# Low parts of 22 weight blocks of a two-layer hybrid trunk: formed by transfers that add into SBUF instead of subtractions on VectorE, with a new order of issue

## The chip, the cores and the metric

The kernel runs on one core of one Trainium2 chip. The metric is the device time of one execution in microseconds (us). Engines are named as in the profile: PE is TensorE's matmuls and PEld its weight loads, DVE is VectorE, ACT is ScalarE, POOL is GpSimd, SP is SyncE, which here only issues transfers. SBUF is the core's working memory, PSUM the eight banks in which PE accumulates, HBM the chip's main memory.

## The reference

Two layers over x of 1024 positions by 1024 channels, in float32. Shortened:

```python
for l in range(2):
    h = rmsnorm(x, attn_norm[l])
    proj = h @ w_in[l]            # one projection, columns split among four mixers
    (c_q, c_kv, k_r, g_b, g_c, u_conv, u_pool, q_sw, k_sw, v_sw) = split(proj)
    y_a = mla_attention(c_q, c_kv, k_r, ..., w_uq[l], w_ukv[l])   # 4 heads, causal, rotary
    y_b = short_gated_conv(g_b, g_c, u_conv, conv_w[l])           # width 3
    y_c = multiscale_pool(u_pool, pool_w[l], pool_scale[l])       # windows 2, 4, 8, 16
    y_d = swa_sink_attention(q_sw, k_sw, v_sw, sinks[l], slopes)  # window 128, ALiBi
    mixed = rmsnorm of each of the four, times mix_norm[l]
    x = x + mixed @ w_o[l]
    gate, up = split(rmsnorm(x, ffn_norm[l]) @ w_gate_up[l])
    x = x + (silu(gate) * up) @ w_down[l]
return rmsnorm(x, final_norm)
```

## The kernel before

**Three matmuls for one.** PE multiplies operands of the rounded format fp32r. To keep float32 accuracy every operand is held as two fp32r tiles, `hi` (the value rounded) and `lo` (the value minus `hi`), and `mm3` (L289) issues three matmuls for each product: hi·hi, hi·lo and lo·hi. For activations `split` makes the pair: `hi` by an ACT copy (L305), `lo` by a DVE subtraction (L306). L308 and L309 are the same with a gain multiplied in.

**Weights of the mixers.** `weights` (L220) loads one block of w_in (128x1024, 512 KB) or w_o (128x768, 384 KB) from HBM, forms `hi` with an ACT copy (L237) and `lo` with a DVE subtraction (L238). Small blocks (up to 256 columns) take a pool of their own. `expect_layer` lists the blocks of a layer in the order in which they will be needed, `ahead` fetches the next one and `take` hands it out. Each block's two tiles stand in a ring of two blocks. The weights of the feed-forward part (`w_gate_up`, `w_down`) go other ways: a factored scheme of sums and differences of blocks, whose sums are formed by POOL (L172) and DVE.

**Stages of one layer.** Input projection; the mixers (their scores in banks `ps_s`, their outputs in `ps_pv`, transposes in `ps_t`); `values` (from L1131 on), which computes MLA's v from its latent, copies it out of `ps_mm` as hi (ACT, L1155) and lo (DVE, L1156); output projection; feed-forward. Layer 0 takes the profile's stretch from 0 to about 1050 us with its mixers up to about 410, layer 1 from 1050 on with its mixers up to about 1410.

**The last stage.** At the very end of layer 1 the down projection's last unit accumulates four 128-row tiles, in two halves of 256 columns, in four banks (two `ps_t`, two `ps_mm`). `evac` (L1882) adds each finished half to x on DVE. The program writes the first half of all four and then the second half of all four.

**What sets the order.** The program's order is not the order of issue. At the end `order_engines` groups the instructions by PSUM bank and engine, gives each group a rank from the place in the program plus a number from the table `MOVES`, and fixes the order of every engine (SP's and POOL's transfer queues too) by that rank. Every engine then runs its list strictly in that order and waits at an instruction whose inputs are not ready.

**Buffers.** SBUF tiles named `u` are 47 places of 128x1024 that go round; the number behind a name in a listing (u7_131) is place and allocation. So a tile can also have to wait until the place's last reader is done.

Of the kernel before, what the change touches and what calls it, by code (L numbers as in the profile page):

```python
# [122 lines left out]
def trunk_kernel(ctx: ExitStack, tc: tile.TileContext, ins, out):  # L123
# [84 lines left out]

    def ring_next():

        if len(ring) == 2:
            ring_drop()
        ring.append((R.pair(), R.pair()))
        return ring[-1]
# [2 lines left out]
        for i in ring.popleft():  # L217
            R.free_pair(i)

    def weights(src, n, between=None):  # L220
        cuts = [slice(0, n // 2), slice(n // 2, n)] if between else [slice(0, n)]
        if n > 2 * P:
            s = F.pair()
            raw = F.ap2(s)
            if between:
                between()
            for c in cuts:
                sp.dma_start(raw[:, c], src[:, c])
            hi, lo = (R.ap2(i) for i in ring_next())
            F.free_pair(s)  # L230
        else:
            raw = wpool.tile([P, 2 * P], F32, name="vraw", tag="vraw")
            sp.dma_start(raw[:, :n], src)
            hi = wpool.tile([P, 2 * P], F32R, name="vhi", tag="vhi")
            lo = wpool.tile([P, 2 * P], F32R, name="vlo", tag="vlo")
# [23 lines left out]
    def expect_layer(l):  # L259
        for m in (2, 3, 0, 4, 5, 6, 1, 13, 14, 10, 11, 12, None, 7, 8, 9) if l == 0 else (14, 10, 11, 12, None, 7, 8, 9):  # L260
            if m is None:
                expect(rope_weights, l)
            else:
                begin = [first_loads] if (l, m) == (0, 2) else []
                expect(weights, ins["w_in"][l, m], 2 * HT, *begin)
        for d in range(NK):
            expect(weights, ins["w_o"][l, d], 6 * P)

    def ahead():
        if stream and not fetched:  # L270
            f, args = stream.popleft()
            fetched.append(f(*args))

    def take():
        ahead()
        return fetched.popleft()

    def pair_weights(src):
# [1859 lines left out]
def arrange(steps, rank=lambda v: v.rank):  # L2138
# [138 lines left out]
    return out  # L2277

MOVES = {
# [63 lines left out]
}  # L2343


# [161 lines left out]
```

## Time and profile before

| | |
|---|---|
| device time, median of 3 runs | 2034.13 us (2032.77 to 2035.87) |
| span of the profiled execution | 2031.1 us, first to last instruction |
| PE | 2014.0 us busy, 9378 matmuls |
| DVE | 1644.2 us busy |
| ACT | 1030.7 us busy |
| POOL | 210.7 us busy |
| transfers | 320.21 MB, mean 158 GB/s |
| granted TensorE clock | 0.998 |

The profiled execution is one of its own; its device time is not listed apart from its span, and the runs' median lies 3.0 us above that span. The profile's rows name engine, line, operation and tiles (out<-in) with buffer numbers left out. A row "PE ps_mm L294 <- DVE u L1156: 2.6, 2, 1.8" in the list of waits says that PE's matmuls of L294 into a bank ps_mm waited for the DVE instruction of L1156, 2.6 us in total, twice, 1.8 at the longest. Line numbers are those of the kernel before; in the changed kernel the same lines stand 16 further down (L294 is L310, L305 is L321, L1882 is L1898), except that L237 and L238 become L252 and L253.

### The profile page before, as it was taken

How to read it: one execution, taken by the hardware profiler on the slowest of the kernel's cores; microseconds unless marked ns; L12 is line 12 of the kernel's file. 1: busy time of each engine (PE TensorE's matmuls, PEld its weight loads, DVE VectorE, ACT ScalarE, POOL GpSimd, SP SyncE). 2: the span in 40 equal slices, each digit the busy share in tenths (PEclk: the TensorE clock that was granted, in tenths of full speed). 3: DMA queues.
4: the chain of work that ended last, by engine and by line, in shares of the span. 5: the costliest groups of instructions: out<-in, count | busy, mean ns of one | idle time of the engine just before them, and what ended most of it. 6: DMA issues, size and time to landing. Idle time of an engine off the chain costs nothing.

```text
span 2031.1 us, 26457 instructions
## 1 busy us (share of the span) xinstructions
PE 2014.0 (99%) x9378; PEld 1669.4 (82%) x9378; DVE 1644.2 (81%) x2793; ACT 1030.7 (51%) x1803; POOL 210.7 (10%) x212
## 2 busy tenths in 40 slices
PE   9999999999999999999999999999999999999998
PEld 7887888878888888888888878888888888888887
DVE  7889989998888888655778999899977777886555
ACT  7447656763333335443545676667333233355342
POOL 0000000013212213000000000000322222220000
PEclk9999999999999999999999999999999999999999
DMA  5100223346666667875455112231644454497652
GB/s 185 55 27 34 75 87 111 126 141 228 211 217 228 217 232 256 304 241 174 148 176 167 39 41 99 89 127 58 218 161 145 159 182 147 157 325 261 198 175 88
DMA packets 163781, 320.21 MB, mean 158 GB/s; under 512 B 13248, under 2 KB 85056, under 8 KB 163648
## 3 DMA queue, kind: packets, MB, share of 16 engines
q1 hardware_dynamic: 163648, 318.51, 45.6%
q8 instruction: 74, 1.21, 0.2%
q14 instruction: 59, 0.48, 0.1%
HBM read 220.41 MB, written 98.04 MB: 157 GB/s over the span
## 4 chain that ended last, share of the span: by engine, by line
PE 93%; DVE 3%; ACT 2%; DMA 1%; issue 1%; SPq 0%; DVEq 0%; ACTq 0%
PE ps_mm L294 37%; PE ps_s L294 28%; PE ps_t L294 11%; PE ps_pv L294 8%; PE ps_pv L1289 2%; PE ps_t L1277 2%; PE ps_s L1223 1%; PE ps_s L1224 1%; PE ps_s L1225 1%; PE ps_pv L814 1%; PE ps_s L753 1%; PE ps_mm L1109 1%; PE ps_t L802 1%; DVE u L346 1%; DVE u L306 1%
## 5 line engine op out<-in xcount | busy, mean ns | idle before, releaser
L294 PE MATMUL ps_mm<-u,u 128*128 128x512 f32 (+1 forms) x3402 | 856.6, 388 | 2.3 <-ACT u L237 1.3
L294 PEld LDWEIGHTS ps_mm<-u,u 128*128 128x128 f32 x3402 | 621.7, 188 | 126.8 <-issue 3.1
L294 PE MATMUL ps_s<-u,u 128*128 128x512 f32 x2628 | 651.2, 389 | 0.0
L294 PEld LDWEIGHTS ps_s<-u,u 128*128 128x128 f32 x2628 | 492.6, 188 | 104.2 <-DVE te L1796 0.8
L305 ACT CAST u<-u 128x1024 fp32r<-128x1024 f32 (+2 forms) x400 | 344.3, 883 | 412.1 <-PE ps_s L294 82.1
L306 DVE TENSOR_TENSOR u<-u,u 128x1024 fp32r<-128x1024 f32 (+2 forms) x400 | 412.7, 1049 | 165.2 <-ACT u L305 127.3
L172 POOL TENSOR_TENSOR u<-u 128x256 f32<-128x256 f32 x176 | 204.3, 1162 | 743.0 <-DMA u<-in_w_dn 239.2
L294 PE MATMUL ps_t<-u,u 128*128 128x512 f32 (+1 forms) x1142 | 275.1, 378 | 1.2 <-ACT u L305 0.8
L294 PEld LDWEIGHTS ps_t<-u,u 128*128 128x128 f32 x1142 | 205.5, 188 | 42.1 <-DVE u L306 1.3
L294 PE MATMUL ps_pv<-u,u 128*128 128x512 f32 x696 | 172.9, 389 | 0.0
L294 PEld LDWEIGHTS ps_pv<-u,u 128*128 128x128 f32 x696 | 130.5, 188 | 27.5 <-ACT tn L458 0.3
L1604 ACT ACTIVATE tp<-tp 128x512 f32<-128x512 f32 x84 | 53.3, 634 | 117.1 <-DVE tp L372 116.8
L1286 POOL MEMSET u<- 128x128 f32 x32 | 6.2, 220 | 858.8 <-DVE te L372 623.7
L305 ACT CAST u<-ps_t 128x512 fp32r<-128x512 f32 (+4 forms) x136 | 64.9, 507 | 58.7 <-PE ps_t L1277 34.1
L306 DVE TENSOR_TENSOR u<-ps_t,u 128x512 fp32r<-128x512 f32 (+4 forms) x136 | 77.0, 584 | 13.6 <-ACT u L305 12.7
L308 ACT ACTIVATE u<-u,par 128x512 fp32r<-128x512 f32 x100 | 70.0, 719 | 34.0 <-DVE u L372 10.9
L309 DVE SCALAR_TENSOR_TENSOR u<-u,par,u 128x512 fp32r<-128x512 f32 x100 | 73.1, 752 | 4.5 <-ACT u L308 4.4
L1605 DVE TENSOR_TENSOR tp<-tp,u 128x512 f32<-128x512 f32 x84 | 62.6, 745 | 13.2 <-ACT tp L1604 12.7
L340 ACT ACTIVATE tn<-u 128x512 f32<-128x512 f32 (+1 forms) x92 | 53.3, 594 | 39.0 <-DVE u L1882 30.2
L458 ACT COPY tn<-ps_s 128x512 f32<-128x512 f32 x66 | 38.4, 582 | 62.8 <-PE ps_s L294 62.5
L372 DVE TENSOR_TENSOR tp<-tp,u 128x512 f32<-128x512 f32 x80 | 60.9, 761 | 1.1
L1289 PE MATMUL ps_pv<-u,u 128*128 128x512 f32 (+2 forms) x184 | 54.4, 358 | 0.0
(220 smaller groups left out, 2171.9 us busy)
## 6 DMA issues: line engine op xcount, KB each, us to landing
u<-in_w_gu SPq DMA_DIRECT2D x88, 512.0 KB, 3.6
ad<-u SPq DMA_DIRECT2D x154, 256.0 KB, 2.8
u<-ad SPq DMA_DIRECT2D x70, 512.0 KB, 4.9
u<-in_w_dn SPq DMA_DIRECT2D x68, 512.0 KB, 4.9
qd<-u SPq DMA_DIRECT2D x44, 512.0 KB, 3.0
u<-qd SPq DMA_DIRECT2D x32, 512.0 KB, 4.9
u<-in_w_in SPq DMA_DIRECT2D x29, 512.0 KB, 3.5
u<-ws SPq DMA_DIRECT2D x28, 512.0 KB, 3.5
```

Of the source, the lines that this page charges most:

```text
L172: pool.tensor_tensor(out=o, in0=o, in1=u, op=ALU.add)
L294: pe.matmul(o, w, r, start=start and k == 0 and i == 0, stop=stop and k == n - 1 and i == 2, skip_group_check=again,)
L305: act.copy(hi, f)
L306: dve.tensor_tensor(out=lo, in0=f, in1=rd(hi), op=ALU.subtract)
L308: act.activation(hi, f, AF.Copy, scale=gain)
L309: dve.scalar_tensor_tensor(out=lo, in0=f, scalar=gain, in1=rd(hi), op0=ALU.mult, op1=ALU.subtract)
L340: act.activation(q, f, AF.Square)
L372: dve.tensor_tensor(out=o, in0=a, in1=b, op=ALU.mult)
L1277: pe.transpose(p[:, b * P : (b + 1) * P], pr[b][j // 4][:, (j % 4) * P : (j % 4 + 1) * P], ident,)
L1289: pe.matmul(py[:, c0:], v_of(j, h), R.ap(s)[:, c0:], start=j == 0 and n == 0, stop=j == nj - 1 and n == 1,)
L1604: last_silu = act.activation(g, g, AF.Silu)
L1605: dve.tensor_tensor(out=g, in0=g, in1=r, op=ALU.mult)
```

## The change

For 22 of the blocks that `weights` makes, `lo_left` takes the place of copy and subtraction. ACT copies the loaded block to `hi`, as before. Then ACT writes minus `hi` over the loaded block (`raw`). POOL's queue issues a transfer that reads the block from HBM again and adds it into `raw`, which then holds the value minus `hi`. SP's queue issues a transfer from `raw` to the tile `lo`. The waits between these four steps are by semaphores; the instruction that waits is POOL's issue (on ACT), SP's issue (on the adding transfer) and PE's matmul (on the copying transfer). The 22 blocks are eight of w_in of layer 0, two of w_in of layer 1, and of w_o the blocks d = 2 to 7 of both layers. The ring now holds one block more than those fetched and not handed out, and `ahead` may fetch two when more than seven places are free.

```diff
     def ring_next():
-        if len(ring) == 2:
+        while len(ring) > len(fetched) + 1:
             ring_drop()
...
+    def lo_left(src, raw, hi, lo, n):
+        act.copy(hi[:, :n], raw[:, :n])
+        act.activation(raw[:, :n], rd(hi[:, :n]), AF.Copy, scale=-1.0)
+        pool.dma_start(raw[:, :n], src, accum_op=ALU.add)
+        sp.dma_start(rd(lo[:, :n]), raw[:, :n])
+
-    def weights(src, n, between=None):
+    def weights(src, n, between=None, on_chip=False):
         cuts = [slice(0, n // 2), slice(n // 2, n)] if between else [slice(0, n)]
+        if n > 2 * P and not on_chip:
+            s = F.pair()
+            raw = F.ap2(s)
+            sp.dma_start(raw[:, :n], src)
+            hi, lo = (R.ap2(i) for i in ring_next())
+            F.free_pair(s)
+            lo_left(src, raw, hi, lo, n)
+            return hi, lo
...
-                expect(weights, ins["w_in"][l, m], 2 * HT, *begin)
+                expect(weights, ins["w_in"][l, m], 2 * HT, begin, m not in (0, 4, 5, 6, 1, 13, 14, 10))
         for d in range(NK):
-            expect(weights, ins["w_o"][l, d], 6 * P)
+            expect(weights, ins["w_o"][l, d], 6 * P, None, d < 2)
 
     def ahead():
-        if stream and not fetched:
+        while stream and (not fetched or len(fetched) < 2 and len(slots.places) > 7):
             f, args = stream.popleft()
             fetched.append(f(*args))
 
     def take():
-        ahead()
+        if not fetched:
+            ahead()
         return fetched.popleft()
...
 MOVES = {
-    3: -1110, 4: -1104, 5: -984, 7: -776, 8: -1105, 14: -914, 15: -964, 16: -307, 18: -279, 20:
+    0: -809, 1: -2, 2: 234, 3: -1340, 4: -1290, 5: -1134, 6: 506, 7: 34, 8: -1130, 9: -443, 10: 398,
```

The table `MOVES` is new from end to end, with several times as many entries. What it moves is seen in the orders of issue. In the rows below stand the line, the operation, the tile written <- the tiles read, the shape, and how many alike follow one another.

Place B, the start of layer 1, block m = 14 of w_in. ACT before; u32_10018 is the loaded block, u16_10020 its hi:

```order
L458 COPY tn_9858<-ps_mm_9843 128x512
L308 ACTIVATE u31_9993<-u14_9757,par_75 128x512
L830 COPY tn_9838<-ps_pv_9786 64x256
L305 CAST u11_9897<-ps_t_9892 128x512
L237 CAST u16_10020<-u32_10018 128x1024
L776 ACTIVATE tp_9940,sm2_9937<-ps_s_9931,sm2_9936 128x256 x2
```

ACT now, with u15_10046 the loaded block and u23_10048 its hi:

```order
L846 COPY tn_9866<-ps_pv_9814 64x256
L222 CAST u23_10048<-u15_10046 128x1024
L474 COPY tn_9886<-ps_mm_9871 128x512
L223 ACTIVATE u15_10046<-u23_10048 128x1024
L846 COPY tn_9866<-ps_pv_9814 64x256
```

The negation stands behind a copy out of the bank ps_mm, and SP's copy of the low part, u14_10049, among loads:

```order
L1060 DMA u13_9785<-in_rope_k 128x512
L232 DMA u7_10054<-in_w_in 128x1024
L995 DMA u13_9785<-xs_85 128x512
L225 DMA u14_10049<-u15_10046 128x1024
L243 DMA u43_10062<-in_w_in 128x1024
L995 DMA u13_9785<-xs_85 128x512
L225 DMA u36_10057<-u7_10054 128x1024
```

On PE the low part of that block, u11_10021 before, is first read here:

```order
L294 MATMUL ps_mm_9725<-u22_9174,u37_9856 128x512 x3
L294 MATMUL ps_mm_10030<-u4_8420,u16_10020 128x512 x2
L294 MATMUL ps_mm_10030<-u4_8420,u11_10021 128x512
L294 MATMUL ps_mm_10030<-u28_8660,u16_10020 128x512 x2
L294 MATMUL ps_mm_10030<-u28_8660,u11_10021 128x512
```

and now here, behind six matmuls of the sliding-window scores and two of another block with the high part:

```order
L310 MATMUL ps_mm_10068<-u12_8448,u23_10048 128x512 x2
L769 MATMUL ps_s_10145<-u46_10005,u37_9396 128x128
L769 MATMUL ps_s_10145<-u26_10006,u37_9396 128x128
L769 MATMUL ps_s_10299<-u46_10005,u37_9396 128x256
L769 MATMUL ps_s_10299<-u26_10006,u37_9396 128x256
L769 MATMUL ps_s_10173<-u46_10005,u37_9396 128x256
L769 MATMUL ps_s_10173<-u26_10006,u37_9396 128x256
L310 MATMUL ps_mm_10093<-u42_10021,u23_10048 128x512 x2
L310 MATMUL ps_mm_10068<-u12_8448,u14_10049 128x512
```

The matmuls with the high part and the first one with the low part, neighbours before, are now eight matmuls apart.

Place A, the output projection of layer 1, ACT now (before, one L237 stood there alone); u4_11638 is the loaded block, u34_11640 its hi:

```order
L321 CAST u15_11607<-ps_t_11605 128x128
L222 CAST u34_11640<-u4_11638 128x768
L1320 COPY tn_11614<-ps_pv_11537 64x512
L321 CAST u30_11778<-ps_t_11773 128x512
L223 ACTIVATE u4_11638<-u34_11640 128x768
```

Copy and negation are two steps apart, and the negation is what POOL's transfer waits for. The last matmul into ps_pv_11537 is the one that the COPY of L1320 waits for; PE's first use of the low part u7_11641 comes 55 matmuls behind it.

The last stage, PE before, where the first half of the bank ps_t_16744 ends:

```order
L294 MATMUL ps_t_16744<-u37_17571,u32_17588 128x256 x3
L358 MATMUL ps_pv_17697<-u1_16955,ones_77 128x512
L294 MATMUL ps_t_16802<-u43_17436,u39_17640 128x256
L294 MATMUL ps_t_16802<-u12_17437,u39_17640 128x256
L294 MATMUL ps_t_16802<-u43_17436,u13_17642 128x256
```

and now, where the same bank is called ps_t_16788 (a half's sum begins with u21_17480 and ends with u6_17615):

```order
L310 MATMUL ps_t_16788<-u6_17615,u13_17632 128x256 x2
L374 MATMUL ps_pv_17741<-u35_16999,ones_77 128x512
L310 MATMUL ps_t_16788<-u6_17615,u13_17632 128x256
L310 MATMUL ps_t_16788<-u21_17480,u45_17631 128x256
L310 MATMUL ps_t_16788<-u44_17481,u45_17631 128x256
```

Before, the next 99 matmuls went to the other three banks before this bank's second half began; now the second half begins at once. The bank ps_t_16846 (ps_t_16802 before) has the same. The two banks ps_mm keep three other halves between theirs.

More of the change, by code (lines that the diff above doesn't have):

```diff
@@ L263, in expect_layer @@
             else:
-                begin = [first_loads] if (l, m) == (0, 2) else []
-                expect(weights, ins["w_in"][l, m], 2 * HT, *begin)
+                begin = first_loads if (l, m) == (0, 2) else None
+                expect(weights, ins["w_in"][l, m], 2 * HT, begin, m not in (0, 4, 5, 6, 1, 13, 14, 10))
         for d in range(NK):
-            expect(weights, ins["w_o"][l, d], 6 * P)
+            expect(weights, ins["w_o"][l, d], 6 * P, None, d < 2)
     def ahead():
-        if stream and not fetched:
+        while stream and (not fetched or len(fetched) < 2 and len(slots.places) > 7):
             f, args = stream.popleft()
```

444 rows, old and new, of the table MOVES are left out of this document.

## The prediction

> **What bounds the kernel now.** The page's first part was read first, then the list of waits of TensorE, then the table by stage, and last the single lines and transfers that the change touches. The columns of the first part are busy time, share of the span and instructions.
>
> ```profile
> span 2031.1 us, 26457 instructions
> PE 2014.0 (99%) x9378; PEld 1669.4 (82%) x9378; DVE 1644.2 (81%) x2793; ACT 1030.7 (51%) x1803; POOL 210.7 (10%) x212
> ```
>
> TensorE (PE) is busy for 2014.0 of 2031.1 us and the number of its matmuls does not change. Time can only be won where PE waits, or lost where it is made to wait anew. The list of its waits (total, times, longest) is short:
>
> ```profile
> PE ps_mm L294 <- DVE u L1156: 2.6, 2, 1.8
> PE ps_mm L294 <- ACT u L237: 1.3, 1, 1.3
> PE ps_pv L198 <- DVE ones L145: 1.1, 1, 1.1
> PE ps_mm L294 <- ACT u L305: 1.0, 1, 1.0
> PE ps_t L294 <- ACT u L305: 0.8, 1, 0.8
> PE ps_s L360 <- ACT tn L1961: 0.5, 1, 0.5
> PE ps_t L294 <- DVE u L306: 0.3, 1, 0.3
> PE ps_s L1223 <- ACT u L305: 0.3, 1, 0.3
> ```
>
> They sum to 7.9 us. L198 and L237 (2.4 us) are the start, before the first data is there, and L1961 (0.5) is the very end; the change touches none of these three. So 5.0 us (2.6 + 1.0 + 0.8 + 0.3 + 0.3) is the most that a relieved VectorE (DVE) or ScalarE (ACT) can give back. The table by stage (first the stretch, then its length and the busy time of PE, PEld, DVE, ACT, POOL) shows where DVE is tight: in the mixers, which is where the 22 blocks are.
>
> ```profile
> 150.00:230.00 80.00, 78.21 (x365) 62.65 (x364) 76.35 (x147) 60.70 (x120) 0.35 (x2) 1.00 0.12 42
> 230.00:410.00 180.00, 180.00 (x897) 149.89 (x896) 165.28 (x360) 121.82 (x259) 2.69 (x14) 1.00 0.30 104
> 1050.00:1200.00 150.00, 149.97 (x740) 123.35 (x739) 132.90 (x321) 94.15 (x214) 0.00 (x0) 1.00 0.30 95
> 1200.00:1230.00 30.00, 28.88 (x139) 23.38 (x138) 29.88 (x62) 20.81 (x46) 0.35 (x2) 1.00 0.17 57
> ```
>
> DVE is 92 to 99% busy there, and yet PE loses almost nothing: 0.00 of 180 us, 0.03 of 150. The granted clock is 1.00, so nothing is to be won there.
>
> **Removed and added, engine by engine.** Ten of the blocks are 128x1024, twelve 128x768.
>
> ```profile
> L237 ACT CAST u<-u x39: 607/1037/1058, 6.2 to 1327.5; 128x1024 fp32r<-128x1024 f32 x21, 128x768 fp32r<-128x768 f32 x16, 128x512 fp32r<-128x512 f32 x2
> L238 DVE TENSOR_TENSOR u<-u,u x39: 685/1215/1228, 7.3 to 1328.4; 128x1024 fp32r<-128x1024 f32 x21, 128x768 fp32r<-128x768 f32 x16, 128x512 fp32r<-128x512 f32 x2
> L308 ACT ACTIVATE u<-u,par 128x512 fp32r<-128x512 f32 x100 | 70.0, 719 | 34.0 <-DVE u L372 10.9
> ```
>
> The durations are ns, shortest, median and longest. DVE loses 10 subtractions of 1.22 us and 12 of about 0.95 (between the 0.685 of 512 columns and the 1.215 of 1024): 23.6 us. ACT gains 22 negations. A 512-wide ACTIVATE takes 0.719 against 0.607 for the CAST of that width, so 0.11 more than a CAST: 10 x 1.15 + 12 x 0.93 = 22.7 us. Neither enters the sum as such. What covers them is PE's own work, 180.00 of 180 us in the second row of the table; ACT has 58 us to spare there. If DVE had been what PE waits for, the 23.6 us would show, but only 5.0 us of waits exist. The 5.0 us are at places (L1156, the split of v, for the most part) whose order, matmul then copy then subtraction then matmul, is the same after the change; I take the gain there as 0, with 5.0 as its bound. The new order might also let a wait of this kind in elsewhere; the largest that exists, 1.8 us, is my bound on that side.
>
> **The new path of a low part.** Before it was load, copy on ACT, subtraction on DVE (1.2 us), use. Now it is load, copy, negation on ACT, a second transfer of the block from HBM that adds into the negated copy (POOL's queue), a third transfer from SBUF to SBUF (SP's queue), use. The prices of the nearest transfers (size, median us from issue to landing):
>
> ```profile
> u<-in_w_in SPq DMA_DIRECT2D x29, 512.0 KB, 3.5
> u<-in_w_o SPq DMA_DIRECT2D x16, 384.0 KB, 3.1
> u<-in_w_kr SPq DMA_DIRECT2D x2, 256.0 KB, 2.6
> u<-in_xT SPq DMA_DIRECT2D x16, 256.0 KB, 5.4
> u<-in_w_in SPq DMA_DIRECT2D x2, 256.0 KB, 6.2
> L172 POOL TENSOR_TENSOR u<-u x176: 729/1072/2930, 432.7 to 1811.7; 128x256 f32<-128x256 f32 x176
> ```
>
> The third transfer is taken at the price of a load, 3.5 us (512 KB) or 3.1 (384 KB). The accumulating one has no row in this trace. From below it is bounded by the same plain loads, 3.1 and 3.5; from above by the dearest loads of a loaded queue, 6.2 at half the size, and I let the range run to 7. It has to read a second stream, the negated copy. From 256 to 512 KB a load grows by 0.9 us (2.6 to 3.5), so 512 KB more cost 1.8 and 384 KB more 1.35: 5.3 and 4.45. POOL, which issues it, has its instructions lengthened by 0.34 us in the median next to a busy DVE (1.072 against the shortest, 0.729); with that I take 5.7 and 4.8, near the middle of the bounds.
>
> The Trainium skill speaks against this change more strongly. Its page "SBUF — State Buffer" (the warning on the "DVE blocks DMA" trap in the section on the doors) says that descriptors of a transfer issued from GpSimd's queue are made by that engine's cores and cannot be written while a DVE operation holds the port pair that the two share. That POOL's additions stretch to 2.9 us agrees in kind, but no run here has such a transfer. By that rule the result is the second rival below.
>
> **Where the price meets PE.** What matters is the lead: the PE work between the end of a negation and the first matmul that uses the low part. Four rows price that work: the first two columns are start and duration.
>
> ```profile
> 1979.82 7.64 PE L294 MATMUL ps_pv<-u,u 128*128 128x512 f32 x33
> 1987.30 4.12 PE L294 MATMUL ps_t<-u,u 128*128 128x256 f32 x33
> 1991.25 1.02 PE L358 MATMUL ps_pv<-u,ones 128*128 128x512 f32 x2
> 1991.45 0.42 DVE L1882 TENSOR_TENSOR u<-u,ps_t 128x256 f32<-128x256 f32 x1 [1.20 <-PE ps_t L294]
> ```
>
> 33 matmuls of 512 columns start 7.48 us apart from the next group, 0.227 each; 33 of 256 take 3.95 to the next start, 0.120 each. With these I counted the lead of all 22 blocks along the new order. Eleven have more than 12 us and drop out, since 5.7 + 3.5 = 9.2 is under it. The short ones:
> - Place B, start of layer 1 (u15_10046, 512 KB). The negation follows a COPY of ps_mm for which PE waits at its next matmul on that bank. From there to the first use of u14_10049 PE has 12 matmuls of 512 (2.72 us) and 38 mixed ones (6.05), 8.8 in all; minus 1.1 for the negation 7.7; minus 3.5 for the third transfer, 4.2 are left for the accumulation. At 5.7 PE waits 1.5 us.
> - Place C, the very first such block (u7_131). ACT's cast of u34_334 comes right behind its negation, and from the matmul that reads u34_334 to the use of u9_134 PE has 38 matmuls of 0.227, 8.6 us; with the cast (0.6) and the signal 9.4; minus 3.5, 5.9 are left. Transfers at the start are slower: 256 KB of x take 5.4 us against 2.6 for as much later. Half of that 2.8 on top of 5.7 makes 7.1: PE waits 1.2 us.
> - Place A and its like, output projection (u4_11638, 384 KB): 55 matmuls, 11.0 us, from the last ps_pv matmul before it; minus 2.2 for the COPY, a cast and the negation on ACT, 8.8; minus 3.1, 5.7 are left against a price of 4.8. No wait. The tightest of these blocks (u39_2461) has 8.2 − 3.1 = 5.1; the others 5.5 to 7.1.
>
> All other transfers are hidden by such leads; their added traffic, 22 x about 1 MB in some 700 us of mixers, meets queues that are 0.12 to 0.30 busy in the table above.
>
> **The tail.** This term needs no new price. In the last stage the order before runs both banks' first column halves before any second half. The new order puts the second half (256 columns) of a ps_t bank directly behind its first half, twice. The second half's first matmul must wait until DVE has evacuated the first. By the rows above: the next matmul starts 1991.25 today; the evacuation ends at 1991.45 + 0.42 = 1991.87. The way from DVE's end to PE's start is read here:
>
> ```profile
> 223.13 0.42 DVE L1156 TENSOR_TENSOR u<-ps_mm,u 128x256 fp32r<-128x256 f32 x1
> 223.69 0.36 PE L294 MATMUL ps_mm<-vhi,u 128*128 128x256 f32 x1 [1.79 <-DVE u L1156]
> ```
>
> 223.69 − 223.55 = 0.14, so PE would start at 1992.01 and loses 0.76 us; twice 1.5 us. (In the first of the two the matmul of L374 stands one matmul ahead of the end of the first half, so it fills nothing.)
>
> **The sum.** 0 for the relieved engines, 1.5 (B) + 1.2 (C) + 0 (A) + 1.5 (tail) = +4.2 us. The profiled execution has a span of 2031.1, which becomes 2035.3; the median of the runs, 2034.13, lies 3.0 above that span for what is around it, so the time is 2038.4. About 0.2% (4.1 us: 2030.1 to 2038.2) is what a measurement of this kernel can tell from no change, and the forecast stands just outside.
>
> **Rivals.**
> - The accumulation is cheap, 4.2 us or less at either size. Then B and C are hidden and only the tail is left: 2035.6, no measurable change. For it: loads of this size take 3.1 to 3.5. Against it: the second stream. Chance 0.24.
> - The accumulation is dear, 7 us at either size, as where POOL is held up by DVE by more than the median. Then B costs 2.8, C 2.5, u39_2461 1.9, and the eight other short leads 0.2 to 1.5 each, 7 together: 14.2 + 1.5 tail = 15.7, 2049.8. For it: DVE 92 to 99% busy where these transfers start, and POOL's longest at 2.9. Against it: L172's median is only 0.34 over its shortest. At 6.2 it is about half. Chance 0.22. (This is where the skill's rule leads.)
> - The relieved DVE removes the waits on L1156, L305 and L306, all 5.0 us, and the transfers stay hidden: −5.0 + 1.5 = 2030.6; if the tail's waits fall away as well, 2029.1. It decides for a gain only if over 4.1 us net are won, that is if nearly every listed wait goes. For it: DVE at 29.88 of 30 us where two of these waits lie. Against it: the longest wait is a chain through PE, ACT and DVE in turn that 23.6 us of DVE work elsewhere do not shorten. Chance 0.18, and some of it falls within 0.2%.
>
> The forecast itself, 2036 to 2044, has 0.36, 0.10 of it below 2038.2. Faster by over 0.2% then gets 0.16 (most of the last rival), the same 0.36 (0.24 + 0.10 + 0.02 of the last rival), slower 0.48 (0.26 + 0.22). The range runs from 2030.0, a little past the last rival's 2030.6, to 2052.0, a little past the dear case.
>
> **What the profile after would show.** A row of accumulating transfers on POOL's queue with 4 to 7 us to landing, the median over all 22 decides between the cases. In the waits of PE, L1898 (the evacuation, L1882 before) with two waits of about 0.7 us near 1990 to 2010; if it is missing, the tail's term is wrong. A wait of PE on a transfer (the copy of L225) near 35 us and at about 1090 us; many of them along 250 to 400 and 1250 to 1400 us would mean the dear case. DVE's total should drop to about 1621, ACT's rise to about 1053. The forecast fails if the wait on L1172 (L1156 before) goes, or if a load queued on SP behind a waiting third transfer comes late: the row of ACT at place B that reads the x chunk u13_9785 is the first in line for that, since its load is issued behind the copy of u14_10049.

## The result and the profile after

The changed kernel takes 2071.4 us (median of 4 runs, 2068.3 to 2075.5) against 2033.5 for the kernel before: 1.018 times as long, 95% interval 1.017 to 1.020. The forecast was 2038.4 with a range up to 2052.0. The profiled execution has a span of 2070.9 us, 39.8 more than before. Its page begins:

```profile
span 2070.9 us, 26523 instructions
PE 2029.4 (98%) x9378; PEld 1667.3 (81%) x9378; DVE 1631.0 (79%) x2771; ACT 1046.1 (51%) x1825; POOL 223.8 (11%) x234
```

DVE lost 13.2 us of work and ACT gained 15.4 (the forecast had DVE at about 1621 and ACT at about 1053). PE does the same 9378 matmuls. What grew is the list of PE's waits, from 8 rows with 7.9 us to 21 rows with 32; here are those that matter (total, times, longest):

```profile
PE ps_s L310 <- ACT u L321: 5.5, 6, 1.5
PE ps_t L310 <- ACT u L321: 4.9, 7, 2.9
PE ps_mm L310 <- ACT u L324: 2.6, 2, 2.3
PE ps_s L769 <- DVE u L648: 2.5, 1, 2.5
PE ps_mm L310 <- DMA u<-u: 2.4, 3, 1.5
PE ps_mm L310 <- DVE u L1172: 2.0, 2, 1.1
...
PE ps_t L310 <- DVE u L1898: 1.0, 2, 0.5
```

Only 2.4 us of them are waits for a low part from the new copying transfer (`u<-u`): three waits, at 260, 1308 and 1349 us, all in the output projections and none at the two places near 35 and 1090 us where the forecast had them. Nearly half of the 32 us name L321, the ordinary split of any operand on ACT, and these are spread over the whole program. The list by stretch (length, then busy time of PE, PEld, DVE, ACT, POOL) shows that the first feed-forward stage, in which the change puts no transfer of its own, lost time as well. The kernel before:

```profile
460.00:810.00 350.00, 349.98 (x1543) 289.09 (x1542) 298.63 (x404) 141.18 (x190) 85.75 (x75) 1.00 0.67 227
810.00:1050.00 240.00, 240.00 (x1063) 198.63 (x1062) 156.94 (x204) 113.65 (x160) 4.08 (x4) 1.00 0.63 213
```

The changed kernel, ten microseconds later:

```profile
470.00:820.00 350.00, 346.27 (x1516) 283.31 (x1515) 290.63 (x392) 137.12 (x185) 79.55 (x72) 1.00 0.65 218
820.00:1060.00 240.00, 237.20 (x1042) 194.57 (x1041) 156.79 (x203) 112.97 (x157) 5.62 (x5) 1.00 0.64 213
```

PE was idle for 0.02 of these 590 us before and for 6.53 after, and got through 48 matmuls fewer.

A busy PE hides short waits, so all runs below are also compared by PE's *lost time*, worked out from each trace: the time between the starts of successive matmuls, less the usual interval of that shape (the median in the kernel before: 0.227 us for 512 columns, 0.176 for 384, 0.120 for 256, 0.109 for 128), added up between fixed matmul numbers. Its total grows by 40.1 us, from 27.5 to 67.5, and the span by 39.8. In us, by stage:

| | start (0–400) | mixers 0 (–2100) | feed-forward 0 (–4650) | start of layer 1 (–5200) | mixers 1 (–6650) | feed-forward 1 (–9000) | last stage | all | of it at half clock |
|---|---|---|---|---|---|---|---|---|---|
| before | 5.0 | 10.0 | 0.6 | 1.1 | 9.4 | −0.2 | 1.6 | 27.5 | 0 |
| changed | 9.1 | 11.1 | 11.3 | 13.6 | 13.1 | 6.0 | 3.2 | 67.5 | 4.0 |
| e1 order new, low parts by DVE | 7.4 | 14.4 | 14.5 | 5.7 | 12.1 | 7.9 | 3.2 | 65.2 | 0 |
| e5 order new, low parts free | 6.5 | 9.6 | 12.4 | 5.1 | 9.7 | 6.8 | 3.2 | 53.3 | 0 |
| e4 transfers do not add | 6.3 | 10.0 | 10.5 | 6.5 | 10.6 | 8.4 | 3.2 | 55.5 | 0 |
| e2 feed-forward order old | 8.2 | 12.3 | 1.1 | 9.8 | 19.1 | −0.5 | 1.6 | 51.7 | 4.5 |
| e3 as e2, low parts by DVE | 7.7 | 14.7 | 1.2 | 5.6 | 16.4 | −0.3 | 1.6 | 46.9 | 0 |
| e7 three blocks by DVE | 8.5 | 12.0 | 12.5 | 6.8 | 13.2 | 7.4 | 3.2 | 63.6 | 1.5 |
| e6 order old, 22 transfers | 17.2 | 31.3 | 0.3 | 15.3 | 24.2 | −0.7 | 1.6 | 89.2 | 13.7 |
| e8 order old, 14 transfers | 8.7 | 12.2 | 1.2 | 1.3 | 16.3 | −0.4 | 1.6 | 41.0 | 4.4 |
| e9 order old, doubled copies | 5.1 | 11.0 | 6.9 | 1.2 | 11.3 | −0.1 | 1.6 | 37.0 | 0 |
| e10 order new, doubled copies | 8.9 | 11.6 | 25.7 | 12.8 | 18.4 | 14.0 | 3.2 | 94.6 | 8.9 |

Each row is one execution, so differences of a few us in a stage can be chance. The first 37 matmuls alone, which wait for the first data ahead of any new transfer, lose between 4.2 and 6.8 us. The last column is a part that the lists of waits do not show. In half of these traces the granted clock reads 0.5 for 3.4 us or a multiple of that, and matmuls of 512 columns then start 0.427 us apart instead of 0.227. All 20 such stretches begin 2 to 5 us behind the beginning of a wait that cost PE 2.0 us or more; some waits of that size have none behind them.

The accumulating transfers themselves (size, median us to landing):

```profile
u<-in_w_in POOLq DMA_DIRECT2D x10, 512.0 KB, 6.7
u<-u SPq DMA_DIRECT2D x10, 512.0 KB, 3.2
u<-in_w_o POOLq DMA_DIRECT2D x12, 384.0 KB, 5.8
u<-u SPq DMA_DIRECT2D x12, 384.0 KB, 2.8
```

They are 1.0 us dearer than forecast at either size. That alone, by the forecast's own working, would have been some 3 us more.

### The profile page after: what moved, and what is told of

The parts are those of the page before. It is cut to its first block, busy times and chain, and to the rows that moved or that the text cites. A ratio compares the mean times of both kernels' runs of the same rounds, so it can differ in the third digit from the quotient of the medians.

```text
span 2070.9 us, 26523 instructions
## 1 busy us (share of the span) xinstructions
PE 2029.4 (98%) x9378; PEld 1667.3 (81%) x9378; DVE 1631.0 (79%) x2771; ACT 1046.1 (51%) x1825; POOL 223.8 (11%) x234
## 5 line engine op out<-in xcount | busy, mean ns | idle before, releaser
L310 PE MATMUL ps_s<-u,u 128*128 128x512 f32 x2628 | 666.8, 391 | 5.7 <-ACT u L321 5.5
L321 ACT CAST u<-u 128x1024 fp32r<-128x1024 f32 (+2 forms) x400 | 344.0, 880 | 455.4 <-PE ps_s L310 91.6
L322 DVE TENSOR_TENSOR u<-u,u 128x1024 fp32r<-128x1024 f32 (+2 forms) x400 | 407.0, 1037 | 149.8 <-ACT u L321 116.8
L310 PE MATMUL ps_t<-u,u 128*128 128x512 f32 (+1 forms) x1142 | 281.5, 379 | 3.2 <-ACT u L321 2.0
L172 POOL TENSOR_TENSOR u<-u 128x256 f32<-128x256 f32 x176 | 198.0, 1127 | 771.6 <-DMA u<-in_w_dn 506.1
L310 PE MATMUL ps_pv<-u,u 128*128 128x512 f32 x696 | 181.1, 390 | 2.0 <-ACT u L321 1.2
L321 ACT CAST u<-ps_t 128x512 fp32r<-128x512 f32 (+4 forms) x136 | 64.8, 506 | 50.0 <-PE ps_t L1293 26.4
L324 ACT ACTIVATE u<-u,par 128x512 fp32r<-128x512 f32 x100 | 69.7, 717 | 34.9 <-DVE u L388 12.8
L325 DVE SCALAR_TENSOR_TENSOR u<-u,par,u 128x512 fp32r<-128x512 f32 x100 | 72.8, 745 | 8.4 <-ACT u L324 8.4
L474 ACT COPY tn<-ps_mm 128x512 f32<-128x512 f32 x52 | 30.5, 586 | 44.2 <-PE ps_mm L310 40.3
```

The costliest lines, as they stand in the source:

```text
L172: pool.tensor_tensor(out=o, in0=o, in1=u, op=ALU.add)
L310: pe.matmul(o, w, r, start=start and k == 0 and i == 0, stop=stop and k == n - 1 and i == 2, skip_group_check=again,)
L321: act.copy(hi, f)
L322: dve.tensor_tensor(out=lo, in0=f, in1=rd(hi), op=ALU.subtract)
L324: act.activation(hi, f, AF.Copy, scale=gain)
L325: dve.scalar_tensor_tensor(out=lo, in0=f, scalar=gain, in1=rd(hi), op0=ALU.mult, op1=ALU.subtract)
```

## The experiments

All variants place each instruction explicitly, in the order that the changed kernel (or the one before) has on every engine, so that an edit moves nothing but what it names. The cuts of code below show each edit by what it does to the program; the lists of places are left out.

**Is it the transfers or the order?** e1 puts the 22 subtractions back on DVE and leaves everything else where the change put it.

```diff
-        act.activation(raw[:, :n], rd(hi[:, :n]), AF.Copy, scale=-1.0)
-        pool.dma_start(raw[:, :n], src, accum_op=ALU.add)
-        sp.dma_start(rd(lo[:, :n]), raw[:, :n])
+        dve.tensor_tensor(out=lo[:, c], in0=raw[:, c], in1=rd(hi[:, c]), op=ALU.subtract)
```

> All 22 low parts formed by DVE subtractions again, each at the place in DVE's order where the copying transfer stood on SP's; negations and both transfers are gone; every other instruction of every engine stands in the changed kernel's order. Theory 1 (late low parts: the accumulating transfers, 6.7 us at 512 KB and 5.8 at 384 KB against 5.7 and 4.8 in the prediction, make PE wait, and the waits in the feed-forward stages follow from them): nearly everything comes back, 2034 to 2042 us. Theory 2 (the new order costs by itself, in stages that have no such transfer too): PE's lost time in the two feed-forward stages, about 19 of the 39 us, stays, and the time is 2052 to 2058.

Measured: 2069.5 us, ratio 1.018 (1.017 to 1.020). Without a single one of the transfers the kernel is as slow as with them. Theory 1 falls. Theory 2's number was missed as well: the table shows that the start of layer 1 recovers 8.0 us and the start 1.7, but the mixers of layer 0 and the two feed-forward stages lose 3.3, 3.2 and 1.9 more. The subtractions, some 23 us of work on DVE, came back into an order that was planned without them; what they cost there shows against e5 below.

e2 keeps the transfers and puts the two feed-forward stages and the last one into the order of before:

```diff
-    place = new_order[step]
+    place = old_order[step] if 3300 <= step < 7700 or step >= 9806 else new_order[step]
```

> The changed kernel with its 22 transfers, but the instructions of both feed-forward stages (the first from a little behind its start to a little ahead of its end, the second with the last stage, as a whole) in the order of the kernel before; the mixers keep the new order. Theory 1: the feed-forward stages only hand on lateness, so 2066 to 2072. Theory 2: the 19 us lost there come back, 2050 to 2056, and PE's waits on L1898 in the last stage are gone.

Measured: 2059.6 us, ratio 1.013 (1.012 to 1.015). The lost time of the two feed-forward stages and the last one goes from 20.5 to 2.2 us (2.0 in the kernel before). So these 18 us are the order's and not lateness handed on. The total falls by 12 and not by 18 because where the two orders are joined, at the end of mixers 1, 6.0 us are lost anew. Of these 5.3 stand at matmuls 6200 to 6400, where the change of order lies and where neither kernel loses over 0.9, so they belong to the splice.

> Both edits: low parts by DVE, feed-forward stages in the order of before; left of the change is the order of issue in the mixers. Theory 1: 2034 to 2040, as the first of these runs. Theory 2: the two gains add, 2034 to 2042; were the mixers' new order itself slow, it would be 2045 or more.

Measured: 2053.2 us, ratio 1.010 (1.008 to 1.011), with the same 18 us back. Against the kernel before 2.7 us are left at the start, 4.7 in mixers 0, 4.5 at the start of layer 1 and 6.9 in mixers 1 with the splice, so the two gains do not add up to it.

**The order with nothing else.** In e5 neither path is paid for; SP copies the loaded block instead.

```diff
-        act.activation(raw[:, :n], rd(hi[:, :n]), AF.Copy, scale=-1.0)
-        pool.dma_start(raw[:, :n], src, accum_op=ALU.add)
         sp.dma_start(rd(lo[:, :n]), raw[:, :n])
```

> The changed kernel's order, with neither path paid for: no subtraction, no negation, no accumulating transfer; SP copies the loaded block itself to the low part's tile, at the place of its old copy, waiting for the load alone (the low parts hold the block). It leaves the new order by itself. Theory 3 (the new order costs some 20 us by itself, and on top of it each of the two ways to form the low parts costs some 15, since the order leaves no slack for either): 2050 to 2058. Rival (the order costs it all, the way of forming low parts nothing): 2066 to 2071.

Measured: 2060.1 us, ratio 1.014 (1.012 to 1.015), 2 us above theory 3's range and 6 under the rival's. Lost time 53.3 us: of the 40.1 us that the change adds, 25.8 are the order's alone (11.8 in feed-forward 0, 7.0 in feed-forward 1, 4.1 at the start of layer 1, 1.5 at the start, 1.5 in the last stage, nothing in the mixers), and 14.2 come with the transfers (2.7 at the start, 1.5 and 3.5 in the mixers, 8.5 at the start of layer 1, a gain of 1.9 in the feed-forward stages). The subtractions cost 11.9 in the same order (e1 less e5). By the medians of the runs the order costs 27.5 of 37.9 us, the transfers 10 and the subtractions 9.5. So the order alone is the larger part, and either way of forming the low parts adds some 10 to 14. Its list of waits is that of the changed kernel without the rows for the transfers:

```profile
PE ps_s L315 <- ACT u L326: 5.9, 6, 1.7
PE ps_t L315 <- ACT u L326: 2.2, 5, 0.7
PE ps_mm L315 <- DVE u L1177: 2.0, 2, 1.1
PE ps_mm L315 <- DMA u<-ws: 1.7, 1, 1.7
```

(L326 there is the split, L321 above.)

**What makes the transfers dear.** e4 has POOL load the block without adding.

```diff
-        pool.dma_start(raw[:, :n], src, accum_op=ALU.add)
+        pool.dma_start(raw[:, :n], src)
```

> The changed kernel in its own order; POOL's 22 transfers load the block and do not add it to the negated copy, so the low parts hold the block itself. If the adding is what makes them dear, they land in 3.5 to 4.5 us after the issue and PE's waits in the mixers shrink by 10 us or more, to 2055 to 2062. If it is the issue from POOL's queue (the descriptors), the median stays at 6 to 6.7 us and the time at 2068 to 2073.

Measured: 2064.1 us, ratio 1.015 (1.014 to 1.017), between the two forecasts, as the transfers' 4.8 and 4.2 us are.

```profile
u<-in_w_in SPq DMA_DIRECT2D x29, 512.0 KB, 3.6
u<-in_w_o SPq DMA_DIRECT2D x16, 384.0 KB, 3.1
u<-in_w_in POOLq DMA_DIRECT2D x10, 512.0 KB, 4.8
u<-in_w_o POOLq DMA_DIRECT2D x12, 384.0 KB, 4.2
```

The price falls into three parts: a load from SP's queue 3.6 and 3.1, POOL's queue instead 1.2 and 1.1 more, the adding 1.9 and 1.6 more. The forecast had 1.8 and 1.35 for the second stream, and 0.4 and 0.35 for the queue. Both parts matter. At 4.8 and 4.2 us most of what the transfers cost is gone: by the profiles nearly all (lost time 55.5 against 53.3 in e5), by the medians of the runs about two thirds (from 2071.4 to 2064.1, with e5 at 2060.1). The Trainium skill's page "SBUF — State Buffer" (the warning on the "DVE blocks DMA" trap) would put the queue's share down to DVE keeping GpSimd's cores from writing descriptors; no run here had the transfers with an idle DVE, so that is left open, and the larger share, the adding, is not in it.

**Are the short leads the place?** e7 forms three blocks on DVE again, the first and the two at the start of layer 1.

```diff
+DVE_LO = ((0, 0), (1, 14), (1, 10))
```

> The changed kernel in its own order with three of its 22 blocks, the first one (place C) and the two at the start of layer 1 (place B and the next), formed by DVE again. The prediction's step that few short leads carry the transfers' cost: 7 us of PE's waits around 1100 to 1150 us and some 3 at the start go, 2060 to 2064. If DVE is too full there, the subtractions take as much as they give, and it stays at 2068 to 2072.

Measured: 2070.9 us, ratio 1.019 (1.017 to 1.021). The start of layer 1 wins the 6.8 us expected, the start only 0.6, and the other stages lose 3.5 more; in the runs nothing is left of it. The start of layer 1 costs 8.5 us (changed less e5) without one wait of PE for a low part: the copy lands at 1132.72 and PE's first use comes at 1133.20, 12.9 us behind the negation where the forecast had 7.7, since PE had been held up before. What came late were loads. The changed kernel there, POOL's queue and then SP's (start, duration):

```profile
1120.81 0.89 POOL L224 DMA_DIRECT2D u<-in_w_in  x1 [290.42 <-DMA vraw<-in_w_ukv]
```

```profile
1121.17 0.33 SPq L1060 DMA_DIRECT2D u<-in_rope_k  x1
1122.45 0.49 SPq L232 DMA_DIRECT2D u<-in_w_in  x1
1123.25 0.47 SPq L995 DMA_DIRECT2D u<-xs  x1
1129.56 0.47 SPq L225 DMA_DIRECT2D u<-u  x1
1135.39 0.33 SPq L995 DMA_DIRECT2D u<-xs  x1
```

The accumulating transfer lands 8.6 us after its issue. The three loads issued within 2.5 us of it (a rotary table, a block, a chunk of x) land after 8.1, 8.1 and 7.9 us; the same three after 4.4, 4.5 and 4.3 in e5, which has no such transfer, and after 5.9, 5.9 and 5.7 in e4, where it does not add. DVE waits for the first of them, ACT for the third and for the next chunk of x, and PE for both:

```profile
DVE u L388 <- DMA u<-in_rope_k: 4.2, 1, 4.2
ACT u L324 <- DMA u<-xs: 7.9, 2, 5.3
```

```profile
1131.91 0.96 PE L769 MATMUL ps_s<-u,u 128*128 128x128 f32 x6 [2.52 <-DVE u L648]
1145.74 0.80 PE L310 MATMUL ps_t<-u 128*128 128x512 f32 x1 [2.90 <-ACT u L321]
```

The second chunk of x, at 1135.39, does stand behind the copy of 1129.56 in SP's queue, but that is not what held it: the queue was free for it from 1130.7 and waited 4.7 us more for DVE's L325, the last reader of the first chunk, whose place it takes (with the low parts free it waits 4.5 there as well). It then took 6.1 us to land, against 2.7 in e5. During the second wait of PE the granted clock falls to half (the column ahead of the last two):

```profile
1144.30:1151.20 6.90, 5.46 (x15) 4.50 (x16) 6.26 (x24) 3.73 (x13) 0.00 (x0) 0.51 0.01 2
```

The two waits and the 2.6 us lost in this stretch make up 8 of the 8.5 us. Over the whole execution 42 loads and stores of SP's queue overlap one of the 22 transfers; they take 5.1 us in the mean against 4.4 in e5, and all others 4.2 in both.

**The transfers in the old order.** e6 has all 22 of them in the kernel before, e8 only the 14 whose copy is planned over 6 us ahead of PE.

```diff
-    on_chip = m not in (0, 4, 5, 6, 1, 13, 14, 10)          # e6; w_o: d < 2
+    on_chip = (l, m) not in ((0, 5), (0, 6), (0, 1), (0, 13), (0, 14), (0, 10))   # e8; 8 of w_o
```

> The kernel before in its own order and with its own ring of blocks; the same 22 low parts by negation and two transfers, the negation right behind the copy on ACT, the copying transfer in SP's queue where it is planned 7.4 us behind the negation. In that order six of the blocks have PE's first use less than 3 us behind that place, and PE waits there about 15 us in all. Theory 3: 2044 to 2050, far less than the changed kernel, since the feed-forward stages and all long leads cost nothing. Rival (the transfers disturb the loads of all stages): 2060 or more.

Measured: 2092.6 us, ratio 1.029 (1.028 to 1.031). Neither theory: the feed-forward stages, which hold none of the 22 transfers, are untouched (0.3 and −0.7 us), but the mixers and the starts cost 63 us and not 15, of which PE loses 13.7 at half clock. PE's list begins:

```profile
PE ps_mm L309 <- DMA u<-u: 17.0, 2, 12.0
PE ps_s L309 <- DMA u<-u: 7.8, 1, 7.8
PE ps_t L1292 <- DVE u L321: 7.8, 1, 7.8
PE ps_pv L1304 <- DVE u L321: 7.3, 1, 7.3
```

The 12.0 of the first row, at the start of layer 1, step by step, on ACT, POOL, SP and PE:

```profile
1138.29 1.06 ACT L223 ACTIVATE u<-u 128x1024 f32<-128x1024 f32 x1
...
1139.85 0.89 POOL L224 DMA_DIRECT2D u<-in_w_in  x1 [291.19 <-DMA u<-in_w_in]
...
1147.42 0.47 SPq L225 DMA_DIRECT2D u<-u  x1
...
1153.89 7.26 PE L309 MATMUL ps_mm<-u,u 128*128 128x512 f32 x22 [12.02 <-DMA u<-u]
```

From the beginning of the negation to PE's read of the low part 15.6 us pass, 7.6 of them for the accumulating transfer and 6.5 for the copying one. The expectation had counted some 11. The last two rows of the list are transfers too, by way of a place: a load of other weights takes the place in which the loaded block stood, and its issue waits for the copying transfer to land. Near 364 us ACT then waits 6.5 us for that load, and DVE and PE for ACT.

> The kernel before in its own order, with only those 14 of the 22 blocks by transfers whose planned copy stands over 6 us ahead of PE's first use. DVE loses 14 subtractions, about 15 us. Theory 3, and the prediction's step that relieved engines give nothing: 2031 to 2035, no change that can be told. If DVE's fullness is what PE's 5 us of waits in the mixers come from, 2027 to 2030. If the transfers disturb the loads of all stages, 2040 or more.

Measured: 2042.8 us, ratio 1.005 (1.004 to 1.007), 10 us slower. The leads hold, no PE wait names a transfer, and DVE's 15 us less bring nothing. The profiled execution, the slowest of the five, loses 3.8 us more than the kernel before at the start (2.4 of them ahead of the first new transfer), 2.2 in mixers 0 and 6.9 in mixers 1. The largest wait there comes through ACT:

```profile
1276.74 0.47 SPq L225 DMA_DIRECT2D u<-u  x1
```

```profile
1279.68 0.83 ACT L222 CAST u<-u 128x768 fp32r<-128x768 f32 x1 [2.25 <-issue]
1280.54 0.84 ACT L223 ACTIVATE u<-u 128x768 f32<-128x768 f32 x1
1281.29 0.46 ACT L1260 ACTIVATE u<-ps_s,sm 128x256 f32<-128x256 f32 x1
```

```profile
1281.89 0.44 PE L1238 MATMUL ps_s<-u,u 128*128 128x384 f32 x1 [2.64 <-ACT u L1260]
```

The block's high part (L222) goes to the place in which the block before it was loaded. That place comes free only when the copying transfer of 1276.74 has read it; it lands at 1279.32, and L222 starts 2.25 us late. It and the negation stand in ACT's list ahead of the exponential of a score (L1260), and PE waits 2.64 us for what follows from it. That ACT is idle for half of the span does not help at this place. Behind this wait the clock is granted by half for 3.4 us, which costs 1.5 more; the rest of the 6.9 us was not followed up.

**Why the new order loses in stages that the change leaves alone.** From both traces: for each tile (a high or a low part) that PE reads in the two feed-forward stages, the time from the end of the ACT or DVE instruction that wrote it to PE's first read. Before, of 524 such tiles none was under 0.5 us and the median was 17 to 18 us. After, 80 of 522 are under 0.5 us and the median is 8.6 to 8.9. One such place, in feed-forward 0 of the changed kernel: a store of a tile to HBM (`ws<-u`), issued at 651.93 and landed at 659.71. The high part that ACT writes next takes that tile's place, so ACT waits for the store, and PE waits for ACT.

```profile
651.93 0.45 SPq L518 DMA_DIRECT2D ws<-u  x1
```

```profile
659.81 1.99 ACT L321 CAST u<-u 128x1024 fp32r<-128x1024 f32 x2 [5.44 <-DMA ws<-u]
```

```profile
661.86 0.50 PE L310 MATMUL ps_mm<-u,u 128*128 128x512 f32 x1 [1.66 <-ACT u L321]
```

Counted in the same way, the mixers are tight in both orders: 92 of 391 tiles under 0.5 us before and 101 of 373 after. That fits what the 22 transfers cost there in the old order too.

To test whether this slack decides, the same disturbance was given to both kernels: every fourth of the 1024-wide feed-forward splits does its ACT copy twice.

```diff
+            if len(SHOCKS) % 4 == 0:
+                act.copy(R.ap2(h), F.ap2(s))
             split(R.ap2(h), R.ap2(lo), F.ap2(s))
```

> The kernel before, in its own order, with a disturbance: 32 of the 1024-wide ACT copies that split feed-forward operands (every fourth) are done twice in a row, some 31 us more work on ACT, all of it ahead of operands that PE reads. Theory 4 (the old order has its operands ready long before PE reads them in the feed-forward stages, 17 us in the median, the new one often just in time): nothing happens here, 2031 to 2036. Rival (any change of the vector engines' pace shows in either order): 2045 or more.

> The changed kernel in its own order with the same disturbance of 32 doubled copies. Theory 4: where operands come just in time each doubled copy delays PE by up to 1 us; with some 80 of 520 feed-forward operands less than 0.5 us ahead of PE, 10 to 25 us more than the changed kernel, 2081 to 2096. Rival (the slack is not what matters, the loss is at single places of its own): no more than 3 us above it, 2069 to 2074.

Measured: 2042.3 us in the old order (ratio to the kernel before 1.004, 1.003 to 1.006), 8.8 us more, and 2096.4 in the new one (1.031, 1.029 to 1.033), 25.0 more than the changed kernel. ACT's total rose by 28.5 and 33.4 us:

```profile
PE 2015.6 (99%) x9378; PEld 1667.7 (82%) x9378; DVE 1640.8 (80%) x2793; ACT 1059.2 (52%) x1835; POOL 207.6 (10%) x212
```

```profile
PE 2041.0 (97%) x9378; PEld 1669.1 (80%) x9378; DVE 1629.2 (78%) x2771; ACT 1079.5 (51%) x1857; POOL 225.9 (11%) x234
```

The old order is not free of it: it loses 6.3 us more in the first feed-forward stage (6.1 of them up to matmul 3500), 1.0 in mixers 0, 1.9 in mixers 1 and 0.1 in the second feed-forward stage. The new order loses 14.4 and 8.0 us more in its two feed-forward stages and 5.3 in mixers 1, 5.8 of all this at half clock, and in the runs nearly three times as much as the old one. So theory 4 holds in direction and size for the new order (0.4 us above its range), and "nothing happens" was too much for the old one.

## Why the prediction was wrong, step by step

- *"0 for the relieved engines", and "the largest that exists, 1.8 us, is my bound on that side"* for waits that the new order might let in. This is the step that failed. The waits of the kernel before bound what can be won; they bound nothing of what a new order can lose. Of the new order only the leads of the 22 blocks and the tail were looked at, while the table `MOVES` moves instructions on every engine from end to end. Alone the order costs 25.8 us (e5; 27.5 by the medians of the runs), 18.8 of them in feed-forward stages that the prediction did not go through. The half that said that nothing is won from a relieved DVE was right: e8 takes 15 us off DVE in the old order and wins nothing, and with the low parts free (e5) the mixers lose 19.3 us as against 19.4 before. (DVE is less full than the prediction reads: its "92 to 99%" is 89% in the row of 1050 to 1200.)
- *The price of the accumulating transfer, 5.7 and 4.8 us.* Measured 6.7 and 5.8. The second stream was sized right (1.8 and 1.35 forecast, 1.9 and 1.6 measured); POOL's queue was taken at a third of its 1.2 us.
- *Place B, 1.5 us*: 8.5 with the start of layer 1 as a whole (changed less e5), and not by the mechanism named. The accumulation took 8.6 us and not 5.7, but PE came so late itself that it had no wait for the copy. The prediction priced the transfer's own lead and left out the loads in flight beside it. Its last paragraph rightly names the x chunk as the first to come late, but as a load queued behind the copy; the trace shows slower landings and a place not yet free. How much of the 8.5 is chance is open: e2, with the same transfers and from matmul 5000 on the same order, lost 3.6 less between matmuls 5050 and 5200.
- *Place C, 1.2 us*: no such wait. The accumulation took 7.7 us against 7.1 forecast and the copy landed 0.1 us ahead of PE's first use. The start as a whole lost 2.7 us more than in e5, half of it in the first 100 matmuls, ahead of that use (matmul 129); the rest was not followed up.
- *Place A and its like, no wait*: 0.3, 1.5 and 0.6 us, the only waits of PE for copies. At u4_11638 itself PE waited 1.5: the lead (10.6 us) and the accumulation (4.7) were no worse than forecast, but the copy, taken at 3.1, landed 5.5 us after its issue. The two mixers as a whole lost 1.5 and 3.5 us more than in e5. e6 and e8 show another way, in the old order: a block's place that comes free late, and a copy and a negation in ACT's list ahead of an instruction that PE waits for. "58 us to spare" is a sum over a stage and says nothing of such a place.
- *The tail, 1.5 us*: right. The list of waits has L1898 twice, and the last stage lost 1.55 us more in every run with the new order and none with the old. By the list itself each wait is 0.5, since it counts from the end of the modelled matmul.
- *The dear case* (2049.8, all of it by PE waiting for transfers) had the right sign and the wrong mechanism: PE waits for copies 2.4 us in all, and with the adding taken out (e4) the kernel is still at 2064.1.

What stays open is why the new table `MOVES` leaves so little slack; the runs show only that it leaves less, and what that costs.

## What to carry to other kernels

In a kernel whose bound engine is 99% busy, an order of issue is worth as much as the slack it keeps: before judging an edit that reorders everything, compare how long ahead of the bound engine its operands are ready, stage by stage, and not only at the places the edit is about. Price a new transfer not only by its own lead but also by the loads in flight beside it, which landed 4 us later at the start of layer 1, and by the SBUF place that it holds until it has landed. A wait that it causes can cost more than itself when the granted clock falls behind it. And an engine's idle share is no cover for an instruction that stands directly ahead of one the bound engine waits for.

## What the runs showed of the hardware that was not expected

- A transfer that adds into SBUF from POOL's queue lands in 6.7 us for 512 KB and 5.8 for 384 KB (4.7 at the shortest, 8.6 at the longest); the same without adding in 4.8 and 4.2, and from SP's queue in 3.6 and 3.1. Its instruction occupies POOL for 0.86 us.
- A negation in place (ACTIVATE, both sides float32) takes 1.05 us at 1024 columns and 0.84 at 768, about as much as the CAST (1.04 and 0.84), against the 1.15 and 0.93 of the forecast.
- Three loads issued within 2.5 us of an accumulating transfer took 7.9 to 8.1 us to land; the same three took 5.7 to 5.9 beside a transfer that does not add and 4.3 to 4.5 with none.
- After a wait of PE of 2 us or more the granted clock can read 0.5 for 3.4 us, which costs some 1.5 us: the same wait of 2.06 us, at the split of v in layer 0, has such a stretch behind it in e6 and e8 and none in the kernel before.
